# Eight of 16 shift tiles of the first norm by VectorE dots, in a hybrid attention layer on one Trainium2 core

## The chip, the cores and the metric

One core of a Trainium2 chip runs the whole layer in float32. The metric is device time in microseconds, the median of repeated runs. The engines named here are TensorE (PE in the profile; PEld is its weight load), VectorE (DVE), ScalarE (ACT), GpSimd (POOL) and SyncE (SP), whose queue issues nearly all DMAs.

## The reference

One layer over 256 latent tokens `x` and 256 context tokens `ctx`, width 2048. What matters here is the first norm and the projections that read it:

```python
mod = silu(c) @ w_mod + b_mod            # for x; 6 x 2048 columns
mod_c = silu(c_ctx) @ w_mod + b_mod      # for ctx
sh1, sc1, gt1, sh2, sc2, gt2 = split(mod, 6)
csh1, csc1, ... = split(mod_c, 6)
h  = rms_norm(x,   g_attn_pre) * (1 + sc1)  + sh1
hc = rms_norm(ctx, g_attn_pre) * (1 + csc1) + csh1
y  = mixer(h, hc)     # keys, values, queries, gates; window and neighbourhood attention; w_o
x  = x + gt1 * rms_norm(y, g_attn_post)
h  = rms_norm(x, g_ffn_pre) * (1 + sc2) + sh2
x  = x + gt2 * rms_norm(conv_ffn(h), g_ffn_post)
```

There are 10 key heads: 8 of the neighbourhood attention (B) and 2 of the window attention (A). In each, a query scores the latent keys and the context keys together in one softmax. A number added to all scores of a query does not change its softmax; so for a B head, whose keys are not rotated, a vector added to all latent and all context keys alike drops out.

## The kernel before

Features lie on partitions. `xn` holds x and ctx side by side, 16 feature tiles of 128 x 512 (256 latent tokens, 256 of the context). `hh` holds the normed tokens in two float32r parts, high and low (`h[:, 0]`, `h[:, 1]`). A weight block of 128 x 2048 goes from a `raw` buffer (four of them) into a high part `wh` (ScalarE) and a low part `wl` (VectorE), two buffers each; this is `split`, L141 and L145. A product is three matmuls: high by high, high by low, low by high.

**First key pass** (loop over the tiles k, pk of six heads). The scale of the norm is made as it goes: `narrow` multiplies silu(c) by scale tiles `rsc` (pm, L367), `scale_of` turns that into the gain columns `Gc` and the scaled `hh`. The keys are therefore of scaled tokens without shift and without the norm's own factor. `squares` adds up the squares; `pss` and `rstd_of` give the factor `rs`. `scaled_keys` (L306) multiplies the keys by it.

**Second key pass** (k = 0 to 15 again, pk of the last four heads). Weight units `ku` are loaded into `ru` and split, two tiles a unit. Beside it the shift is made, in two ways. `ND` = 4 feature tiles are dots on VectorE: `load_sd` loads a transposed 1 MB tile of `wm_sd` into the buffer `sd`, and `dot` (L481) multiplies it by a row of silu(c) or silu(c_ctx) and adds it up, two dots a tile; L485 adds the bias into `shc`. The first two dots stand in the first pass, at k = 12 and 14, six in the second. The other twelve tiles are a TensorE product `pmsh` (L597), at k = 1, 5, 9, 13, four tiles of `wm_sh` each, evacuated, transposed and added into `shc` at k = 14. At k = 15 TensorE turns `shc` (`ptsd`, L637), and it goes out to `shd`.

In the same pass `xn` is multiplied in place by Gc and rs (L610), and `whole` (L579, L580) then writes the final `hh`, with shift: tiles 0 to 2 inside the pass, the rest after it.

**Values** (L712). Ten weight blocks, four token tiles. Beside them VectorE has 29 dots (`beside`): 20 give the bias of the keys (two per head, L687: the shift of x and of ctx times the key weights `wkt`, a 1 MB block a head), and 9 are further columns of w_mod (`mods`, L244), whose rest follows in the attention, the gates and the output projection. `key_bias` (L673) adds the biases. The rows `shr` that these dots read are loaded from `shd` when the memory of the key passes is free, that is after the last `whole`.

**What sets the order.** The order of TensorE in both key passes is written by hand, and so is SyncE's until k = 12 of the first. All else is laid out by a planner before the run: each engine's queue is then fixed, and it takes the earliest piece of the code that is ready by the planner's own costs. A buffer is loaded again only when its last reader is done.

Of the kernel before, what the change touches and what calls it, by code (L numbers as in the profile page):

```python
# [10 lines left out]
F32 = mybir.dt.float32  # L11
F32R = mybir.dt.float32r
AF = mybir.ActivationFunctionType
ALU = mybir.AluOpType

P = 128
D = 2048
KT = D // P
S = 256
# [15 lines left out]
C_BMOD = 0  # L35
# [4 lines left out]
C_CW = 160  # L40
# [11 lines left out]
NBLK = B_DN + 44  # L52
NK1 = 6
NK2 = NKVA + NHB - NK1
ND = 4
SW = (KT - ND) * P // 4
KW = (NKVA + NHB) * P
J0, NS = 24, 8
# [13 lines left out]
def layer_kernel(ctx, tc, xc, xt, ccol, crow, wm_sc, wm_sd, wm_sh, wm_b, cols, wk, wkt, ws, rope, mask_a, bias_b, out):  # L72
# [46 lines left out]
    x1d = tc.dram_tile([S, D], F32, name="x1d")  # L119
    sild = tc.dram_tile([2 * KT, P], F32, name="sild")  # L120
    ggd = tc.dram_tile([2, KT, P], F32, name="ggd")
    shd = tc.dram_tile([2, D], F32, name="shd")

    nraw = [0]
    nmod = [0]
# [155 lines left out]
    with ExitStack() as mx:  # L281
# [10 lines left out]
        with ExitStack() as at:  # L292
# [30 lines left out]

            st = kv.enter_context(ExitStack())
            hcp = st.enter_context(tc.tile_pool(name="hcp", bufs=1))
            shc = hcp.tile([P, 2, KT], F32, name="shc")
            sp = st.enter_context(tc.tile_pool(name="sp", bufs=1, side="right"))
            xn = sp.tile([P, KT, T2], F32, name="xn")
            ssq = sp.tile([P, T2], F32, tag="ssq", bufs=1, name="ssq")
# [139 lines left out]

            def load_sd(t):  # L470
                if t < ND:
                    rsd[t] = sp.tile([P, D], F32, tag="sd", bufs=1, name=f"sd{t}")
                    sync.dma_start(out=rsd[t], in_=wm_sd[t])

            def dot(after=None):
                t, v = divmod(ndot[0], 2)
                ndot[0] += 1
                with ExitStack() as es:
                    if after:
                        es.enter_context(tc.issue_after(after))  # L480
                    d_ = nc.vector.scalar_tensor_tensor(  # L481
                        out=rsd[t][:] if v else junk, in0=rsd[t][:], scalar=1.0, in1=shrow[v], op0=ALU.mult, op1=ALU.mult,
                        accum_out=sh0[:, t, v : v + 1]).ins
                if v:
                    nc.vector.tensor_scalar(  # L485
                        out=shc[:, :, t], in0=sh0[:, t], scalar1=col[:, C_BMOD + t : C_BMOD + t + 1], scalar2=None, op0=ALU.add)
                    load_sd(t + 1)
                return d_

            def keys(pk, wh, wl, o, k, part=slice(0, 3)):  # L490
# [13 lines left out]
            for k in range(KT):  # L504
# [7 lines left out]
                        load_xn(3, 1)  # L512
                        load_sc(3)
                if k == 2:
                    cr = sp.tile([P, D], F32, tag="sd", bufs=1, name="cr")[: 2 * KT, :P]
                    sync.dma_start(out=cr, in_=crow)
                    nc.scalar.activation(cr, cr, AF.Silu)
                if k == 4:
                    sync.dma_start(out=sild, in_=cr)
                if k in (6, 8):  # L520
                    shrow.append(silu_row(wp, "wl", 2, (k - 6) // 2, F32R))
                if k == 10:
                    load_sd(0)
                if k >= KT - 2:
                    load_unit(k + 2)
                if k == 12:
                    sync.dma_start(out=col[:, C_CW:], in_=cols[:, C_CW:])
                    loads.close()
                if k > 3:
                    units[k + 1] = unit(k + 1)  # L530
                if k == 12:

                    d_ = dot(done_u[k + 1][1])
                    after = squares(14, done_u[k + 1][0], d_)
                    with tc.issue_after(sq_[0]):
                        warm_table(AF.Sqrt, "k", eps[:, 0:1])
                if k == 14:
# [45 lines left out]

            pm = bank("pmsh")
            pk = [acc(f"pk{NK1 + i}") for i in range(NK2)]
            rsh = {q: raw_block(wm_sh[q], (P, 4 * SW)) for q in range(4)}
            for k in range(KT):
                if k % 2 == 0:
                    load_unit(KT + k // 2 + 2)
                    if k + 2 < KT:  # L590
                        units[KT + k // 2 + 1] = unit(KT + k // 2 + 1)
                if k % 4 == 1:
                    keys(pk[0], *units[KT + k // 2], (k % 2) * NK2 * P, k)

                    for q in range(k - 1, k + 3):
                        for j in range(4):
                            nc.tensor.matmul(  # L597
                                pm[32 * j : 32 * j + 32, :SW], cc[:, q, :], rsh[q][:, SW * j : SW * j + SW],
                                start=q == 0, stop=q == KT - 1)
                    for q in range(k + 3, k + 7):  # L600
                        if q < KT:
                            rsh[q] = raw_block(wm_sh[q], (P, 4 * SW))
                if k == KT - 2:
                    split_to(b0)
                    load_to(b0 + 1)
                if k in (2, 3, 6, 7, 10, 11):
                    dot(e_.ins)
                for v in range(2):
                    x_ = xn[:, k, v * S : v * S + S]
                    nc.vector.scalar_tensor_tensor(  # L610
                        out=x_, in0=x_, scalar=Gc[:, k, v : v + 1], in1=rs[:, v * S : v * S + S],
                        op0=ALU.mult, op1=ALU.mult)
                if k > 12:
                    whole(k - 13)
                for i in range(k % 4 == 1, NK2):
                    keys(pk[i], *units[KT + k // 2], (k % 2) * NK2 * P + i * P, k)
                    if k == KT - 2 and i < 2:
                        if i == 0:
                            pt = bank("ptsh")
                        n_ = min(2 * P, SW - 2 * P * i)  # L620
                        ev = up.tile([P, 2 * P], F32, tag="half", bufs=2, name=f"evsh{i}")
                        nc.scalar.activation(ev[:, :n_], pm[:, 2 * P * i : 2 * P * i + n_], AF.Copy)
                        for b in range(0, n_, P):
                            o = 2 * P * i + b
                            nc.tensor.transpose(pt[:, o : o + P], ev[:, b : b + P], ident[:])
                        if i:

                            view = pt[:, :SW].rearrange("p (b j w) -> p j b w", j=4, w=32)
                            bm = col[:, C_BMOD + ND : C_BMOD + KT].rearrange("p (j b) -> p j b", j=4)
                            for v in range(2):  # L630
                                nc.vector.tensor_tensor(
                                    out=shc[:, v, ND:].rearrange("p (j b) -> p j b", j=4), in0=view[:, :, :, v], in1=bm,
                                    op=ALU.add)
                    if k == KT - 1 and i == 2:

                        pt = bank("ptsd")
                        nc.tensor.transpose(pt[: 2 * KT, :P], shc[:].rearrange("p a b -> p (a b)"), ident[:])  # L637
                        ev = up.tile([P, 2 * P], F32, tag="half", bufs=2, name="evsd")
                        nc.scalar.activation(ev[: 2 * KT, :P], pt[: 2 * KT, :P], AF.Copy)
                        sync.dma_start(out=shd.rearrange("v (k p) -> (v k) p", p=P), in_=ev[: 2 * KT, :P])  # L640
            order.close()
            for k in range(3, KT):
                if k in (3, 6):
                    for i in (0, 1) if k == 3 else (2, 3):
                        scaled_keys(NK1 + i, pk[i])
                whole(k)
            st.close()
            ccs.close()

# [10 lines left out]
            shr = []  # L660
            for v in range(2):
                shr.append((cbp, rowp)[v].tile([P, D], F32, tag="row", name=f"shr{v}"))
                sync.dma_start(out=shr[v], in_=shd[v].partition_broadcast(P))
            junk = cbp.tile([P, D], F32, name="junk")
            kb = cbp.tile([P, NKVA + NHB, 2], F32, name="kb")
            rkt = {}
            crb = [None]
            nbeside = [0]

            def key_bias(i):  # L670
                for v in range(2):
                    k_ = of(v, kT[:, i])
                    nc.scalar.activation(k_, k_, AF.Identity, bias=kb[:, i, v : v + 1])  # L673
                if i >= NHB:
                    rope_of(kT[:, i], 1, f"k{i}")

            def beside(n):
                for _ in range(n):
                    n_, v = divmod(nbeside[0], 2)
                    nbeside[0] += 1  # L680
                    if n_ < NKVA + NHB:
                        for q in range(n_, min(n_ + 2, NKVA + NHB)) if v == 0 else ():
                            if q not in rkt:
                                rkt[q] = raw_block(wkt[q])
                        i = n_
                        r = rkt[i]
                        nc.vector.scalar_tensor_tensor(  # L687
                            out=r if v else junk[:], in0=r, scalar=1.0, in1=shr[v][:], op0=ALU.mult, op1=ALU.mult,
                            accum_out=kb[:, i, v : v + 1])
                        if v and n_:  # L690
                            key_bias(n_ - 1)
                    else:
                        if crb[0] is None:
                            key_bias(NKVA + NHB - 1)
# [4 lines left out]
            for c, (n0, nw, per) in enumerate(((0, 512, 4), (512, 512, 4), (1024, 256, 8))):  # L699
                pv = [acc(f"pv{c}_{i}") for i in range(4)]  # L700
                for g in range(KT // per):
                    wh, wl = block(2)
                    for kk in range(per):

                        if nb and kk < (2 if nb == 8 else 3 if nb % 2 else 4):
                            beside(1)
                        k = g * per + kk
                        w = slice(kk * nw, kk * nw + nw)
# [849 lines left out]
```

## The time and the profile before

| | us |
|---|---|
| median of 3 runs (1499.41 to 1499.93) | 1499.61 |
| the profiled execution | 1500.27 |
| its span, first to last instruction | 1498.5 |
| TensorE busy | 1487.1 |
| VectorE busy | 1222.7 |
| ScalarE busy | 811.4 |
| shift product pmsh on TensorE (L597) | 11.1 |

Each row of the page gives an engine's busy time and its share of the span. The chain of waits goes back from the last instruction, at each step to what released it; an engine that owns the chain sets the time. The granted TensorE clock was 0.998. The longest stretches of the chain lie in the up projection (pu) and the down projection (c), which the change does not touch; it touches the first 270 us, and a little of the output projection (py_o, 677 to 765).

### The profile page before, as it was taken

What the parts mean: (1) busy time and instruction counts of PE and PEld (TensorE: products, weight loads), DVE (VectorE), ACT (ScalarE), POOL (GpSimd) and SP (SyncE); (2) the same over time, 40 slices, a digit from 0 to 9 for tenths busy, and PEclk for the clock granted to TensorE, in tenths of its full rate; (3) what the DMA queues carried; (4) which work ended last, traced back from release to release, by engine and by line L of the source; (5) the groups of instructions that cost most, each with busy time, mean ns of one, the idle gap of its engine ahead of it and who ended that gap; (6) DMA issues with size and microseconds to landing.
All of it is one profiled execution on the core that took longest, in us unless ns stands there. A gap on an engine that the chain in (4) does not pass through costs nothing.

```text
span 1498.5 us, 21727 instructions
## 1 busy us (share of the span) xinstructions
PE 1487.1 (99%) x8488; PEld 1279.0 (85%) x8488; DVE 1222.7 (82%) x1861; ACT 811.4 (54%) x1338; POOL 1.8 (0%) x11
## 2 busy tenths in 40 slices
PE   9999999999999999999999999999999999999997
PEld 7876889998888888888888888888888888888886
DVE  4496998989988888877778887887888878887887
ACT  4342542777765544555666555555555555445543
POOL 0000000000000000000000000000000000000000
PEclk9999999999999999999999999999999999999999
DMA  9988789754368888778856666666666654554652
GB/s 367 391 322 337 275 295 353 281 205 168 142 227 305 314 323 322 306 281 340 305 204 222 251 234 241 239 238 225 253 224 226 224 194 168 224 214 185 265 215 108
DMA packets 60551, 382.66 MB, mean 255 GB/s; under 512 B 6560, under 2 KB 8992, under 8 KB 18336
## 3 DMA queue, kind: packets, MB, share of 16 engines
q1 hardware_dynamic: 59728, 380.20, 67.5%
q8 instruction: 67, 1.10, 0.3%
q10 hardware_dynamic: 720, 1.07, 0.2%
q14 instruction: 36, 0.29, 0.1%
HBM read 377.00 MB, written 4.24 MB: 254 GB/s over the span
## 4 chain that ended last, share of the span: by engine, by line
PE 97%; DMA 1%; DVE 1%; ACT 1%; issue 0%; DVEq 0%
PE pu L214 21%; PE c L1318 12%; PE pu L215 11%; PE pk L493 7%; PE pv L712 7%; PE pg L214 7%; PE py_o L943 5%; PE pq L214 4%; PE pb L214 4%; PE pg L215 4%; PE x L1318 3%; PE pq L215 2%; PE pb L215 2%; PE po L853 1%; PE s L822 1%; PE pm L367 1%
## 5 line engine op out<-in xcount | busy, mean ns | idle before, releaser
L145 DVE TENSOR_TENSOR wl<-raw,wh 128x1024 fp32r<-128x1024 f32 (+1 forms) x444 | 520.6, 1201 | 114.3 <-ACT wh L141 113.7
L141 ACT ACTIVATE wh<-raw 128x1024 fp32r<-128x1024 f32 (+1 forms) x444 | 444.4, 1036 | 184.1 <-PE pg L214 54.5
L214 PE MATMUL pu<-h,wh 128*128 128x512 f32 x1404 | 487.6, 390 | 0.0
L215 PE MATMUL pu<-h,wl 128*128 128x256 f32 x1404 | 395.9, 282 | 0.0
L214 PEld LDWEIGHTS pu<-h,wh 128*128 128x128 f32 x1404 | 263.4, 188 | 55.0
L215 PEld LDWEIGHTS pu<-h,wl 128*128 128x128 f32 x1404 | 265.4, 189 | 0.0
L214 PE MATMUL pg<-h,wh 128*128 128x512 f32 x464 | 161.5, 390 | 0.0
L1318 PE MATMUL c<-wh,ff 128*128 128x512 f32 x448 | 138.0, 389 | 0.0
L215 PE MATMUL pg<-h,wl 128*128 128x256 f32 x464 | 130.8, 282 | 0.0
L493 PE MATMUL pk<-h,ku 128*128 128x512 f32 x480 | 118.0, 398 | 0.6 <-DVE ku L145 0.4
L244 DVE SCALAR_TENSOR_TENSOR raw<-raw,crb 128x2048 f32<-128x2048 f32 x48 | 109.6, 2285 | 9.8 <-DMA raw<-in_wm_b_dram 9.3
L219 ACT ACTIVATE half_u<-pu 128x256 f32<-128x256 f32 x88 | 33.6, 384 | 147.8 <-PE pu L215 147.8
L493 PEld LDWEIGHTS pk<-h,ku 128*128 128x128 f32 x480 | 87.4, 188 | 25.3 <-issue 4.8
L214 PE MATMUL pq<-h,wh 128*128 128x512 f32 x304 | 108.7, 396 | 0.0
L214 PEld LDWEIGHTS pg<-h,wh 128*128 128x128 f32 x464 | 87.1, 188 | 18.2
L712 PE MATMUL pv<-wh,h 128*128 128x512 f32 (+1 forms) x384 | 101.6, 354 | 0.0
L1318 PEld LDWEIGHTS c<-wh,ff 128*128 128x128 f32 x448 | 84.1, 188 | 17.4
L214 PE MATMUL pb<-h,wh 128*128 128x512 f32 x256 | 89.4, 390 | 0.0
L215 PEld LDWEIGHTS pg<-h,wl 128*128 128x128 f32 x464 | 87.7, 189 | 0.0
L1318 PE MATMUL c<-wl,ff 128*128 128x512 f32 x224 | 87.3, 390 | 0.0
L215 PE MATMUL pq<-h,wl 128*128 128x256 f32 x304 | 85.5, 281 | 0.0
L943 PE MATMUL py_o<-wh,zz 128*128 128x512 f32 x256 | 78.4, 390 | 0.0
(241 smaller groups left out, 2085.8 us busy)
## 6 DMA issues: line engine op xcount, KB each, us to landing
raw<-in_ws_dram SPq DMA_DIRECT2D x222, 1024.0 KB, 4.8
raw<-in_wm_b_dram SPq DMA_DIRECT2D x64, 1024.0 KB, 4.8
raw<-in_wm_sc_dram SPq DMA_DIRECT2D x15, 1024.0 KB, 7.8
raw<-in_wm_sh_dram SPq DMA_DIRECT2D x16, 768.0 KB, 7.1
raw<-in_wkt_dram SPq DMA_DIRECT2D x10, 1024.0 KB, 6.9
raw<-in_wk_dram SPq DMA_DIRECT2D x7, 768.0 KB, 8.3
crb<-sild SPq DMA_DIRECT2D x4, 1024.0 KB, 7.7
sd<-in_wm_sd_dram SPq DMA_DIRECT2D x4, 1024.0 KB, 8.4
```

Source lines behind the costliest of these rows:

```text
L141: a_ = nc.scalar.activation(hi, src, AF.Copy)
L145: v_ = nc.vector.tensor_tensor(out=lo, in0=src, in1=hi, op=ALU.subtract)
L214: nc.tensor.matmul(pt[:, :], wh[:, w], a, start=first and i == 0, stop=False, skip_group_check=True)
L215: nc.tensor.matmul(pt[:, :S], wl[:, w], a[:, 0], start=False, stop=last and i == n - 1, skip_group_check=True)
L219: a_ = nc.scalar.activation(t[:], pt[:, S:], AF.Copy)
L244: nc.vector.scalar_tensor_tensor(out=r, in0=r, scalar=1.0, in1=row, op0=ALU.mult, op1=ALU.mult, accum_out=modx[:, j : j + 1])
L367: nc.tensor.matmul(pm[32 * j : 32 * j + 32, t * P : t * P + P], cc[:, q, :], rsc[k + t][:, q * P : q * P + P], start=q < 4, stop=q >= KT - ...
L493: nc.tensor.matmul(pk[:], wt[:, w], hh[:, :, k, a], start=k == 0 and a == 0 and wt is wh, stop=k == KT - 1 and a == 1)
L712: nc.tensor.matmul(pv[i][:, :nw], src[:, k, a, t0 : t0 + P], wt[:, w], start=k == 0 and q == 0, stop=k == KT - 1 and q == 2)
L822: nc.tensor.matmul(s_ps, qs[hd][:, a, qt * P : qt * P + P], k_[:, w], start=q == 0, stop=q == 2)
L943: p_ = nc.tensor.matmul(py[t][:], act[:, k, a, t * P : t * P + P], wt[:, w], start=k == 0 and q == 0, stop=k == nk - 1 and q == 2)
L1318: nc.tensor.matmul(pt[:], a(i), wt[:, w], start=k not in begun, stop=stop and q == 2, skip_group_check=True)
```

## The change

- `ND` = 8: eight tiles of the shift are dots, and `pmsh` has 256 columns in place of 384. `sd` has two buffers. Tile 0 is loaded at k = 9 of the first pass, tile 1 at 13, tile 2 before the second pass, and each further tile when the second dot of the tile two before is done. The dots stand at k = 10 (two) and k = 14 of the first pass, and one at each k from 0 to 12 of the second.
- Shift tiles of `wm_sh` are loaded two at a time, 1 MB a load. The load of `cols` moves from k = 12 of the first pass to k = 8 of the second.
- `xn` is multiplied by Gc on ScalarE (two instructions of 256) and by rs on VectorE (one of 512).
- Block 1 of the values is split after whole(9), and not after the last `whole`.
- `shc` and `shd` get a third row: the context's shift less the latent one. B heads get one dot, with this row, and one bias, on the context's keys; A heads keep two dots, the second now with the difference, and the first result is added to it.
- Beside the values are 25 dots: 12 for the keys and 13 of `mods`.

```diff
-ND = 4
+ND = 8
...
-            shc = hcp.tile([P, 2, KT], F32, name="shc")
+            shc = hcp.tile([P, 3, KT], F32, name="shc")
...
-                    rsd[t] = sp.tile([P, D], F32, tag="sd", bufs=1, name=f"sd{t}")
+                    rsd[t] = sp.tile([P, D], F32, tag="sd", bufs=2, name=f"sd{t}")
...
-                    load_sd(t + 1)
+                    if t:
+                        load_sd(t + 2)
...
-                if k == 10:
-                    load_sd(0)
+                if k in (9, 13):
+                    load_sd(k // 13)
...
                 if k == 12:
-                    sync.dma_start(out=col[:, C_CW:], in_=cols[:, C_CW:])
                     loads.close()
...
+                if k == 10:
+                    dot(dot(done_u[k + 1][1]))
                 if k == 12:
-                    d_ = dot(done_u[k + 1][1])
-                    after = squares(14, done_u[k + 1][0], d_)
+                    after = squares(14, *done_u[k + 1])
...
-            rsh = {q: raw_block(wm_sh[q], (P, 4 * SW)) for q in range(4)}
+            rsh = {}
+            def load_sh(k):
+                for q in range(k, min(k + 4, KT), 2):
+                    r = raw_block(wm_sh[q : q + 2].rearrange("k p n -> p k n"), (P, 2, 4 * SW))
+                    rsh[q], rsh[q + 1] = r[:, : 4 * SW], r[:, 4 * SW :]
+            load_sh(0)
+            load_sd(2)
             for k in range(KT):
+                if k == 8:
+                    sync.dma_start(out=col[:, C_CW:], in_=cols[:, C_CW:])
...
-                    for q in range(k + 3, k + 7):
-                        if q < KT:
-                            rsh[q] = raw_block(wm_sh[q], (P, 4 * SW))
+                    load_sh(k + 3)
...
-                if k in (2, 3, 6, 7, 10, 11):
+                if k < 13:
                     dot(e_.ins)
                 for v in range(2):
                     x_ = xn[:, k, v * S : v * S + S]
-                    nc.vector.scalar_tensor_tensor(
-                        out=x_, in0=x_, scalar=Gc[:, k, v : v + 1], in1=rs[:, v * S : v * S + S],
-                        op0=ALU.mult, op1=ALU.mult)
+                    nc.scalar.activation(x_, x_, AF.Copy, scale=Gc[:, k, v : v + 1])
+                nc.vector.tensor_tensor(out=xn[:, k], in0=xn[:, k], in1=rs[:], op=ALU.mult)
...
-                        nc.tensor.transpose(pt[: 2 * KT, :P], shc[:].rearrange("p a b -> p (a b)"), ident[:])
+                        nc.vector.tensor_tensor(out=shc[:, 2], in0=shc[:, 1], in1=shc[:, 0], op=ALU.subtract)
+                        nc.tensor.transpose(pt[: 3 * KT, :P], shc[:].rearrange("p a b -> p (a b)"), ident[:])
...
                 whole(k)
+                if k == 9:
+                    split_to(b0 + 1)
...
-                sync.dma_start(out=shr[v], in_=shd[v].partition_broadcast(P))
+                sync.dma_start(out=shr[v], in_=shd[2 * v].partition_broadcast(P))
...
-                for v in range(2):
+                for v in range(2) if i >= NHB else (1,):
                     k_ = of(v, kT[:, i])
                     nc.scalar.activation(k_, k_, AF.Identity, bias=kb[:, i, v : v + 1])
...
+            jobs = [(i, v) for i in range(NKVA + NHB) for v in ((1,) if i < NHB else (0, 1))]
...
+                        if v and i >= NHB:
+                            nc.vector.tensor_tensor(out=kb[:, i, 1:], in0=kb[:, i, 1:], in1=kb[:, i, :1], op=ALU.add)
...
-                        if nb and kk < (2 if nb == 8 else 3 if nb % 2 else 4):
+                        if nb and kk < (2 if nb > 7 else 3):
                             beside(1)
```

More of the change, by code (lines that the diff above doesn't have):

```diff
@@ L121, in layer_kernel @@
     ggd = tc.dram_tile([2, KT, P], F32, name="ggd")
-    shd = tc.dram_tile([2, D], F32, name="shd")
+    shd = tc.dram_tile([3, D], F32, name="shd")
     nraw = [0]
@@ L485, in dot @@
                     nc.vector.tensor_scalar(
-                        out=shc[:, :, t], in0=sh0[:, t], scalar1=col[:, C_BMOD + t : C_BMOD + t + 1], scalar2=None, op0=ALU.add)
-                    load_sd(t + 1)
+                        out=shc[:, :2, t], in0=sh0[:, t], scalar1=col[:, C_BMOD + t : C_BMOD + t + 1], scalar2=None, op0=ALU.add)
+                    if t:
+                        load_sd(t + 2)
                 return d_
@@ L514, in layer_kernel @@
                 if k == 2:
-                    cr = sp.tile([P, D], F32, tag="sd", bufs=1, name="cr")[: 2 * KT, :P]
+                    cr = sp.tile([P, D], F32, tag="sd", bufs=2, name="cr")[: 2 * KT, :P]
                     sync.dma_start(out=cr, in_=crow)
@@ L616, in layer_kernel @@
                     keys(pk[i], *units[KT + k // 2], (k % 2) * NK2 * P + i * P, k)
-                    if k == KT - 2 and i < 2:
+                    if k == KT - 2 and i < -(-SW // (2 * P)):
                         if i == 0:
@@ L625, in layer_kernel @@
                             nc.tensor.transpose(pt[:, o : o + P], ev[:, b : b + P], ident[:])
-                        if i:
+                        if i == -(-SW // (2 * P)) - 1:
                             view = pt[:, :SW].rearrange("p (b j w) -> p j b w", j=4, w=32)
@@ L636, in layer_kernel @@
                         pt = bank("ptsd")
-                        nc.tensor.transpose(pt[: 2 * KT, :P], shc[:].rearrange("p a b -> p (a b)"), ident[:])
+                        nc.vector.tensor_tensor(out=shc[:, 2], in0=shc[:, 1], in1=shc[:, 0], op=ALU.subtract)
+                        nc.tensor.transpose(pt[: 3 * KT, :P], shc[:].rearrange("p a b -> p (a b)"), ident[:])
                         ev = up.tile([P, 2 * P], F32, tag="half", bufs=2, name="evsd")
-                        nc.scalar.activation(ev[: 2 * KT, :P], pt[: 2 * KT, :P], AF.Copy)
-                        sync.dma_start(out=shd.rearrange("v (k p) -> (v k) p", p=P), in_=ev[: 2 * KT, :P])
+                        nc.scalar.activation(ev[: 3 * KT, :P], pt[: 3 * KT, :P], AF.Copy)
+                        sync.dma_start(out=shd.rearrange("v (k p) -> (v k) p", p=P), in_=ev[: 3 * KT, :P])
             order.close()
@@ L667, in layer_kernel @@
             crb = [None]
-            nbeside = [0]
             def key_bias(i):
-                for v in range(2):
+                for v in range(2) if i >= NHB else (1,):
                     k_ = of(v, kT[:, i])
@@ L675, in key_bias @@
                     rope_of(kT[:, i], 1, f"k{i}")
+            jobs = [(i, v) for i in range(NKVA + NHB) for v in ((1,) if i < NHB else (0, 1))]
             def beside(n):
                 for _ in range(n):
[L679 to L682, printed above, removed]
+                    if jobs:
+                        i, v = jobs.pop(0)
+                        for q in range(i, min(i + 2, NKVA + NHB)):
                             if q not in rkt:
                                 rkt[q] = raw_block(wkt[q])
-                        i = n_
                         r = rkt[i]
@@ L689, in beside @@
                             accum_out=kb[:, i, v : v + 1])
-                        if v and n_:
-                            key_bias(n_ - 1)
+                        if v and i >= NHB:
+                            nc.vector.tensor_tensor(out=kb[:, i, 1:], in0=kb[:, i, 1:], in1=kb[:, i, :1], op=ALU.add)
+                        if v and i:
+                            key_bias(i - 1)
                     else:
```

## The prediction

> **What bounds the kernel now.** I read the page first (engine totals, chain), then the chain piece by piece around the first norm, then busy time by stretch, then VectorE's own timeline, then the loads.
>
> ```profile
> span 1498.5 us, 21727 instructions
> PE 1487.1 (99%) x8488; PEld 1279.0 (85%) x8488; DVE 1222.7 (82%) x1861; ACT 811.4 (54%) x1338; POOL 1.8 (0%) x11
> PE 97%; DMA 1%; DVE 1%; ACT 1%; issue 0%; DVEq 0%
> ```
>
> TensorE is busy for 99% of the span and owns 97% of the chain. So a gain must be TensorE work removed, and a loss must be a new TensorE wait. The sum is against this profiled execution: span 1498.5, 1500.27 us with what lies around it; the median of the three runs is 1499.61, so I add my change to the median.
>
> The chain, in order of time (start, us, what):
>
> ```profile
> 100.79 2.72 PE pmsh L597 x32
> ...
> 153.05 0.11 PE ptsd L637
> 153.16 0.70 PE pk L493 x3
> 153.87 110.09 PE pv L712 x576
> ```
>
> The shift product (pmsh) is four groups of 32 records, 2.72 us each; the first is shown. The second key pass ends and the values begin at 153.87.
>
> Busy time by stretch (TensorE, weight load, VectorE, ScalarE, GpSimd, clock, DMA share, GB/s):
>
> ```profile
> 60.00:80.00 20.00, 20.00 (x203) 16.25 (x202) 9.92 (x20) 9.83 (x17) 0.00 (x0) 1.00 1.01 413
> 88.60:101.25 12.65, 12.65 (x62) 10.05 (x64) 12.65 (x19) 2.98 (x3) 0.00 (x0) 1.00 0.87 328
> 101.25:149.81 48.56, 48.16 (x289) 33.66 (x281) 37.06 (x64) 12.35 (x18) 0.00 (x0) 1.00 0.87 338
> 153.90:263.90 110.00, 110.00 (x577) 95.04 (x576) 97.87 (x108) 42.99 (x73) 0.46 (x2) 1.00 0.83 311
> ```
>
> Four things are to be seen: TensorE waits 0.4 us in the second key pass (48.16 of 48.56); in 60 to 80 the DMA engines are full; VectorE has no gap from 88.6 to 101.25; from there to 149.81 it has 48.56 - 37.06 = 11.5 us to spare. That is what the change spends.
>
> **What it removes from TensorE.** The nearest group of narrower records, in the chain:
>
> ```profile
> 71.60 1.89 PE pm L367 x64
> ```
>
> A group of 32 records takes 2.72 us at 384 columns, and half of a 64-record group takes 0.94 at 128; straight between them, 256 columns take 1.83, so 0.89 a group, 3.6 us for four. One transpose goes (0.11, as ptsd's). The 0.4 us wait may go. Bound: -4.1 us, if nothing new waits.
>
> **What it adds to VectorE in the second key pass.** Durations from start to start in its timeline:
>
> ```profile
> 68.48 0.69 DVE L433 TENSOR_TENSOR ssq<-ssq,sq 128x512 f32<-128x512 f32 x1
> 69.09 0.95 DVE L145 TENSOR_TENSOR ku<-raw,ku 128x768 fp32r<-128x768 f32 x1
> 74.76 0.47 DVE L388 TENSOR_SCALAR Gc<-ptm,col,bgc 128x2 f32<-128x2 f32 x2 [4.72 <-PE ptm L386]
> ...
> 101.25 1.67 DVE L610 SCALAR_TENSOR_TENSOR xn<-xn,Gc,rs 128x256 f32<-128x256 f32 x4
> 102.84 2.29 DVE L481 SCALAR_TENSOR_TENSOR kT<-sd,crb 128x2048 f32<-128x2048 f32 x1
> 105.05 0.08 DVE L481 DVE_READ_ACCUMULATOR kT<-sd,crb 128x1 f32 x1
> ...
> 108.05 1.22 DVE L145 TENSOR_TENSOR ku<-ru,ku 128x1024 fp32r<-128x1024 f32 x1
> 109.19 0.23 DVE L485 TENSOR_SCALAR shc<-sh,col 128x2 f32<-128x2 f32 x1
> 109.32 0.48 DVE L610 SCALAR_TENSOR_TENSOR xn<-xn,Gc,rs 128x256 f32<-128x256 f32 x1
> ```
>
> A dot is 2.21, its column add 0.13, an xn product of 256 is 0.40, a sum of two 512-wide tiles 0.61 (68.48 to 69.09; the nearest row for the new xn product), a 1024-wide split 1.14 (108.05 to 109.19), which is also a wl half. In the second pass there are 13 dots instead of 6: 7 x 2.21 = 15.5; four more column adds: 0.5; 32 products of 0.40 become 16 of 0.61: -3.0; the subtraction for the third row, 0.13, priced as a column add. whole(3), two products of the xn kind and size, ran ahead into this stretch and now falls behind it, as its place in the code says: -0.8. Together +12.3, against 11.5 spare. The stretch ends with the last adds into shc:
>
> ```profile
> 149.65 0.24 DVE L631 TENSOR_TENSOR shc<-ptsh,col 128x12 f32<-128x12 f32 x2 [1.85 <-PE ptsh L625]
> ```
>
> Without one idle moment its work now ends at 101.25 + 37.06 + 12.3 = 150.6.
>
> Who waits for its end: TensorE's order is written by hand, and the ptsd transpose (last unit but one of the pass) reads shc, which needs the last dot and the subtraction. Without a wait TensorE would be there at 153.05 - 4.1 = 148.9. Two more splits can stand ahead of the subtraction: block 0's wl halves, at k = 14 in the code, the subtraction at k = 15. Before, their weights had to wait until the last shift loads freed a buffer; now two 1 MB loads hold what four buffers held, so the weights can come earlier. With both halves ahead the subtraction ends at 152.9, with none at 150.6. I take one, 151.7, for the order is not to be seen before it is laid out. From ptsd to the first value product is 153.87 - 153.05 = 0.82.
>
> **What it does to TensorE in the first key pass.** Tile 0 of wm_sd moves from k = 10 to k = 9, ahead of the xn loads and of scale tiles 12 and 13, in a queue order written by hand:
>
> ```profile
> 52.48 0.52 SPq L250 DMA_DIRECT2D crb<-sild  x1
> 53.05 0.97 SPq L340 DMA_DIRECT2D xn<-in_xc_dram  x2
> ```
>
> Scale tiles 12 and 13 by issue and landing:
>
> ```profile
> L134 SPq DMA_DIRECT2D raw<-in_wm_sc_dram x1: 327/327/327, 59.3 to 59.3; - x1
> ...
> DMA to landing us min/median/max: 9.2/9.2/9.2
> ...
> L134 SPq DMA_DIRECT2D raw<-in_wm_sc_dram x1: 328/328/328, 61.9 to 61.9; - x1
> ...
> DMA to landing us min/median/max: 9.1/9.1/9.1
> ```
>
> They land at 68.5 and 71.0, over 9 us after issue and 2.5 us apart for 1 MB: with the engines full, this queue is bound by bytes, and comes out in order of issue. With 1 MB more ahead, tile 12 lands at 71.0 and tile 13 at 73.5. TensorE needs them at 71.60 and 72.54 (half of the 1.89). So a new wait of about 1.0 us at 72.5, which moves all behind it, pss and VectorE's chain from 88.6 too. Its bounds: 0, if the engines take the loads otherwise, and 2.5, if tile 13 had no slack. [...]
>
> The two dots that now stand at k = 10 cost 4.55 in VectorE's 4.72 us gap before 74.76: hidden, and the wait just named widens the gap; without that cover they would push Gc by 4.55.
>
> **The sum.** Values begin at 151.7 + 1.0 + 0.8 = 153.5, against 153.87: -0.4. Of the 4.1 us saved, 1.0 goes to the load and some 2.7 to ptsd's wait on VectorE.
>
> **Edits at nothing.** ScalarE's 32 extra scalings at 0.40 (VectorE's own xn price) make 12.8 us beside 12.35 busy in 48.56. The cols load moves to k = 8; its first reader there is far behind. Splitting block 1 after whole(9) puts two wl halves 2.3 us earlier among 13 x 0.8 us of whole; TensorE takes 11 us a block (110.09 for ten). Four dots fewer beside the values remove 4 x 2.2 from a VectorE that had 12 us spare and made TensorE wait for nothing in 153.9 to 263.9. But shr's second row now gates the first dot, and its load waits for the last whole, on the VectorE that is now behind; before, in the first of these rows, VectorE idled 3.5 us there for the first row:
>
> ```profile
> 172.39 2.29 DVE L687 SCALAR_TENSOR_TENSOR junk<-raw,shr 128x2048 f32<-128x2048 f32 x1 [3.52 <-DMA shr<-shd]
> 223.40:264.40 41.00, 41.00 (x274) 37.91 (x273) 33.59 (x34) 11.90 (x19) 0.00 (x0) 1.00 0.90 342
> ```
>
> Eight dots now take a fresh 1 MB block each, so a group of values loads four blocks: 4 x 2.5 = 10 us of 11. The stretch from 223.4 in the second row, where each wm_b dot reads a fresh block, is already such a one, and TensorE is busy for all of its 41 us. Four wm_b dots and loads leave the output projection, whose products are in the 99%; nothing is booked. So 1499.61 - 0.4 = 1499.2.
>
> **Rivals.** *VectorE keeps up.* Its order lets the subtraction through in time, because my 0.61 is too dear or work I put ahead of it falls behind. Then only the load's wait stands against the saving: -4.1 + 1.0 = -3.1, 1496.5; without that wait 1495.5. For it: ScalarE idles, and VectorE's order is free to change. Against: 12.3 us in 11.5. Chance 0.25.
>
> *wm_sd comes too late.* With two buffers, a slot is refilled while the other tile's two dots run: 2 x (2.21 + 0.61) + 1.14 + 2 x 0.13 + 0.61 = 7.65 us. The two loads of before in that stretch:
>
> ```profile
> L473 SPq DMA_DIRECT2D sd<-in_wm_sd_dram x2: 328/328/328, 108.2 to 122.1; - x2
> ...
> DMA to landing us min/median/max: 7.4/8.4/9.5
> ```
>
> Five tiles (3 to 7) come so. At 8.4 each waits 0.75, 3.7 in all: 1499.2 + 3.7 = 1502.9, slower; at 9.5 it would be 9. It decides above 8.3 us a load. For it: two of the three loads of a group are still queued behind shift loads. Against: those are 2 MB a group instead of 3, and xn products can fill the gap. Chance 0.15.
>
> *The values become load-bound.* At the 311 GB/s of the values before 4.19 MB take 13.5 us, 2.5 over a block; for three groups +7.5, 1506.7. Against: 413 GB/s were moved from 60 to 80. Chance 0.05. [...]
>
> **How the numbers follow.** Forecast 0.55: VectorE's chain takes back most of the saving; its own range is -2.9 to +2.9 (no half to both halves ahead, the load's wait 0 to 2.5, up to 1 us of idle in the chain). 0.2% is 3.0 us, about what a measurement of this kernel can tell from no change. Faster 0.25, same 0.55, slower 0.20. The range reaches to the first rival's 1495.5 and the second's 1502.9.
>
> **What would show it.** After: a pmsh group of 1.8 us; a TensorE gap near 72.5 ended by a raw load; VectorE without idle time from 88.6 to the subtraction; ptsd waiting 2 to 4 us for it; the first value product near 153.5. I am wrong if ptsd waits under 1 us, if VectorE idles on sd, or if TensorE waits for a wl in the values.

## The result, and the profile after

The changed kernel takes 1509.84 us (median of 4 runs, 1508.79 to 1510.29), the kernel before 1499.51 beside it: a ratio of 1.0068, 95% interval 1.0051 to 1.0085. It is slower by 10.3 us, where I had forecast 1499.2. The profiled execution took 1510.29, with a span of 1508.5.

First the page of the changed kernel, as at the head of the prediction (engine totals, granted TensorE clock in 40 slices, chain):

```profile
span 1508.5 us, 21740 instructions
PE 1488.5 (99%) x8487; PEld 1281.9 (85%) x8487; DVE 1220.8 (81%) x1852; ACT 821.4 (54%) x1361; POOL 1.8 (0%) x11
PEclk9999999899999999999999999999999999999999
PE 92%; DVE 4%; DMA 2%; ACT 1%; issue 1%; DVEq 0%
```

TensorE has less work, and yet it is busy 1.4 us longer: in slice 8 of 40 its clock is not whole. And 8% of the chain are not its own, where it was 3%. The same stretches as before the change:

```profile
60.00:80.00 20.00, 19.17 (x198) 15.31 (x197) 13.60 (x23) 10.35 (x20) 0.00 (x0) 1.00 1.02 414
101.25:149.81 48.56, 46.17 (x294) 33.95 (x293) 48.44 (x61) 15.71 (x26) 0.00 (x0) 1.00 0.91 354
153.90:263.90 110.00, 110.00 (x577) 95.05 (x576) 91.81 (x109) 36.22 (x56) 0.46 (x2) 1.00 0.88 338
223.40:264.40 41.00, 41.00 (x274) 37.93 (x273) 33.14 (x30) 9.90 (x14) 0.00 (x0) 1.00 1.00 402
```

TensorE has the wait in 60 to 80, and one of 2.4 us in the second key pass, where VectorE is now full (48.44 of 48.56). In the values it waits for nothing (110.00 of 110.00), but the DMA engines are full from 223.4 on: 402 GB/s, share 1.00, where it was 342 and 0.90. TensorE's rows at these places:

```profile
73.48 1.08 PE L367 MATMUL pm<-raw,cc 128*32 128x128 f32 x32 [0.83 <-DMA raw<-in_wm_sc_dram]
...
140.98 2.00 PE L608 MATMUL pmsh<-raw,cc 128*32 128x256 f32 x32
142.91 2.56 PE L494 MATMUL pk<-h,ku 128*128 128x512 f32 x10
147.87 0.73 PE L494 MATMUL pk<-h,ku 128*128 128x512 f32 x2 [2.39 <-DVE ku L145]
...
152.77 0.62 PE L724 MATMUL pv<-wh,h 128*128 128x512 f32 x2
...
153.90 0.27 PE L646 MATMUL ptsd<-ident,shc 128*48 128x128 f32 x1
...
263.68 0.39 PE L214 MATMUL pq<-h,wh 128*128 128x512 f32 x1
...
271.73 0.50 PE L214 MATMUL pq<-h,wh 128*128 128x512 f32 x1 [2.33 <-ACT wh L141]
272.99 0.53 PE L215 MATMUL pq<-h,wl 128*128 128x256 f32 x1 [0.76 <-DVE wl L145]
...
284.25 0.48 PE L856 MATMUL pt<-ident,sma 128*128 128x128 f32 x1 [2.96 <-DVE sma L849]
```

Up to the end of the values little is lost: the first query product starts at 263.68, and before the change at 263.80:

```profile
263.80 0.39 PE L214 MATMUL pq<-h,wh 128*128 128x512 f32 x1
```

The whole loss arises in the next 27 us, where the queries take over from the values: 2.33 + 0.76 us of waiting for block 11, 2.96 for the first head's softmax, and behind each gap a stretch at half clock:

```profile
147.80:151.00 3.20, 3.13 (x15) 2.58 (x16) 3.20 (x8) 2.02 (x5) 0.00 (x0) 1.00 1.00 415
272.90:276.50 3.60, 3.52 (x11) 3.03 (x12) 3.60 (x5) 0.24 (x1) 0.00 (x0) 0.53 0.29 89
284.30:290.00 5.70, 5.70 (x18) 4.62 (x19) 5.46 (x7) 5.25 (x10) 0.00 (x0) 0.50 0.48 168
```

3.6 us at 0.53 lose 1.7, 5.7 us at 0.50 lose 2.85 (a 512-column product takes 0.43 us there and 0.23 ahead of the gap): with the 6.05 of gaps 10.6, which is the whole loss and a little more. (Behind the 2.39 us wait at 147.87 the clock stayed at 1.00.)

Why the first gap? ScalarE's timeline, the kernel before and then the changed one:

```profile
263.28 0.74 ACT L717 ACTIVATE vv<-pv 128x256 f32<-128x256 f32 x2
263.92 1.05 ACT L141 ACTIVATE wh<-raw 128x1024 fp32r<-128x1024 f32 x1
264.87 0.38 ACT L717 ACTIVATE vv<-pv 128x256 f32<-128x256 f32 x1
265.13 1.06 ACT L141 ACTIVATE wh<-raw 128x1024 fp32r<-128x1024 f32 x1
...
269.56 0.39 ACT L764 ACTIVATE qb<-pq 128x256 f32<-128x256 f32 x1 [2.85 <-PE pq L215]
...
272.88 1.28 ACT L109 ACT_TABLE_LOAD   x1
```

```profile
262.80 1.46 ACT L729 ACTIVATE vv<-pv 128x256 f32<-128x256 f32 x4 [7.71 <-PE pv L724]
269.44 0.38 ACT L776 ACTIVATE qb<-pq 128x256 f32<-128x256 f32 x1 [5.17 <-PE pq L215]
270.31 0.42 ACT L141 ACTIVATE h<-rq 128x256 fp32r<-128x256 f32 x1 [0.49 <-DVE rq L777]
270.63 1.99 ACT L141 ACTIVATE wh<-raw 128x1024 fp32r<-128x1024 f32 x2
...
281.49 1.28 ACT L844 ACT_TABLE_LOAD   x1
282.79 0.64 ACT L844 ACTIVATE sma<-sma,st 128x416 f32<-128x416 f32 x1
...
283.43 1.99 ACT L141 ACTIVATE wh<-raw 128x1024 fp32r<-128x1024 f32 x2
```

(Blocks are numbered from 0; 0 to 9 are the values', 10, 11 and 12 those of the first three queries.) Before, block 11's split (`wh`, 263.92) stands among the copies of the last values. Now it stands behind `qb`, the copy of the first query, which must wait for TensorE until 269.44; ScalarE idles 5.17 us. Block 12's split (283.43) stands behind the first head's exponential, ahead of which ScalarE loads the table (1.28 us at 281.49, on the path; before, 1.28 at 272.88, in idle time). Yet the two blocks had long landed. Their loads in the trace, before and then after:

```profile
L134 SPq DMA_DIRECT2D raw<-in_ws_dram x1: 327/327/327, 250.7 to 250.7; - x1
...
DMA to landing us min/median/max: 8.8/8.8/8.8
```

```profile
L134 SPq DMA_DIRECT2D raw<-in_ws_dram x1: 328/328/328, 252.9 to 252.9; - x1
...
DMA to landing us min/median/max: 7.6/7.6/7.6
```

Block 11 landed at 259.5 before the change and at 260.5 after. Block 12 was issued at 264.4 before and at 261.0 after; it landed at 270.3 and at 270.5:

```profile
L134 SPq DMA_DIRECT2D raw<-in_ws_dram x1: 328/328/328, 264.4 to 264.4; - x1
...
DMA to landing us min/median/max: 5.9/5.9/5.9
```

```profile
L134 SPq DMA_DIRECT2D raw<-in_ws_dram x1: 350/350/350, 261.0 to 261.0; - x1
...
DMA to landing us min/median/max: 9.5/9.5/9.5
```

So what changed is the order that the planner wrote for ScalarE. Why it wrote this one is not shown; it goes by its own costs, not by the landings above.

### The profile page after: what moved, and what is told of

Same layout as the page of the kernel before. It is cut to its first block, busy times and chain, and to the rows that moved or that the text cites. A ratio compares the mean times of both kernels' runs of the same rounds, so it can differ in the third digit from the quotient of the medians.

```text
span 1508.5 us, 21740 instructions
## 1 busy us (share of the span) xinstructions
PE 1488.5 (99%) x8487; PEld 1281.9 (85%) x8487; DVE 1220.8 (81%) x1852; ACT 821.4 (54%) x1361; POOL 1.8 (0%) x11
## 4 chain that ended last, share of the span: by engine, by line
PE 92%; DVE 4%; DMA 2%; ACT 1%; issue 1%; DVEq 0%
PE pu L214 21%; PE c L1330 12%; PE pu L215 11%; PE pv L724 7%; PE pg L214 7%; PE py_o L955 6%; PE pq L214 5%; PE pb L214 4%; PE pg L215 4%; PE pk L494 3%; PE x L1330 3%; PE pq L215 2%; PE pb L215 2%; PE po L865 1%; PE s L834 1%; PE pt L856 1%
## 5 line engine op out<-in xcount | busy, mean ns | idle before, releaser
L214 PE MATMUL pq<-h,wh 128*128 128x512 f32 x304 | 112.5, 406 | 2.3 <-ACT wh L141 2.3
```

What stands on the lines that cost most here:

```text
L214: nc.tensor.matmul(pt[:, :], wh[:, w], a, start=first and i == 0, stop=False, skip_group_check=True)
```

## The experiments

Theory 1: the 25 dots beside the values read 23 fresh 1 MB blocks (10 of keys, 13 of mods), where the 29 read 19, and this makes the hand-over late. Rival 2: the key passes do it. Rival 3: ScalarE's fixed order is the price, not the loads. Rival 4: it is VectorE's work. (The expectation of e9 calls rival 3 theory 3. Theory 5 and rival 6 are about the clock, rival 7 about the loads of the second key pass.) Each ratio is against runs of the kernel before taken beside it, with medians of 1499.2 to 1499.7.

**Which half of the change.** Passes alone (e1: the changed kernel with the old `key_bias`, job list and counts), values alone (e2: the old kernel with a third row in `shc` and `shd`, and the new dots).

> Both key passes as in the changed kernel (ND = 8, sd0 at k = 9, narrower pmsh), but beside the values the 29 dots of before, two for every B head. Theory 1 (the 25 dots of the values, with three fresh 1 MB blocks a group, make the value and query weights late; the passes are worth -0.3): 1499.2, within 1 us of before, and no TensorE gap over 1 us between 263 and 290. Rival 2 (the passes, or the shift of times that they bring, make the hand-over late): about 1509, with the gaps near 270 and 281 still there.

> The passes of before (ND = 4, pmsh of 384 columns) with the third shift row, and the changed kernel's 25 dots beside the values. Theory 1: the whole loss without the passes, about 1510 (1508 to 1512), gaps near 270 and 281. Rival 2: about 1499.6, no such gaps. If both halves are needed at once, both this and the passes alone stay near 1499.5.

Passes alone: 1501.02, ratio 1.0012 (1.0003 to 1.0020). Values alone: 1507.84, ratio 1.0055 (1.0043 to 1.0068), with waits of 1.42, 0.76 and 2.97 us at the hand-over. So theory 1 holds against rival 2 for some 8 of the 10 us. The passes alone miss their 1499.2 by 1.8 us, but in the profiled execution (1500.42) the passes are not what is late: the first query product starts at 263.06, 0.7 us earlier than before. What they gain goes at the hand-over again, in waits of 0.29 and 1.17 us for block 12, where no gap over 1 us was expected:

```profile
277.42 0.38 PE L215 MATMUL pq<-h,wl 128*128 128x256 f32 x1 [1.17 <-DVE wl L145]
```

There too the block had landed (at 272.5), and its split came at 274.65, behind the second query's copy at 274.37.

**Bytes or dots.** e3 leaves four mods to later, e5 keeps 25 dots but loads fewer blocks, e11 keeps the loads without the dots:

```diff
# e3
-                        if nb and kk < (2 if nb > 7 else 3):
+                        if nb and kk < (1 if nb == 9 else 2 if nb > 4 else 3):
...
# e5; the first of two heads that share a block leaves it unchanged
-                                rkt[q] = raw_block(wkt[q])
+                                rkt[q] = rkt[q - 1] if q % 2 and q < NHB else raw_block(wkt[q])
...
# e11, on top of e3
+                        elif nb and kk < (2 if nb > 7 else 3):
+                            spare.append(raw_block(wkt[0]))
+                            if len(spare) > 1:
+                                nc.vector.tensor_copy(junk[:, :1], spare.pop(0)[:, :1])
...
```

> The changed kernel with 21 dots beside the values instead of 25: two a block from block 5 on and one beside block 9, so four fresh 1 MB blocks fewer in the second half of the values. Theory 1 (bytes make weight blocks 11 and 12 late): 4 MB fewer, some 10 us of loads, so blocks 11 and 12 land in time, both gaps go, 1499 to 1501. Rival 3 (ScalarE's fixed order at the hand-over and not the loads): the order stays, the first gap stays, 1505 to 1510.

> The changed kernel with all its 25 dots, but two neighbourhood heads share one 1 MB key block, so that 19 fresh blocks are loaded beside the values as before, not 23 (left out: half of the heads get the wrong block's bias). Theory 1 (bytes make weight blocks 11 and 12 late): 1499 to 1501, as with 21 dots, though VectorE does as much as in the changed kernel. Rival 4 (VectorE's dots in the values, not the loads, are what got dearer, and 21 dots helped by being fewer): about 1509.

> The kernel with 21 dots beside the values, and in the place of the four dots that it leaves out only their four 1 MB loads, read by copies of one column (VectorE has no more to do than with 21 dots). Theory 1 (fresh blocks that pass through the raw buffers make the hand-over late): the whole loss comes back, 1507 to 1510, with the gaps near 270 and 281. Rival 4 (VectorE's dots): 1499.

21 dots: 1499.05, ratio 0.9998 (0.9989 to 1.0007). 25 dots on 19 blocks: 1499.29, ratio 0.9999 (0.9990 to 1.0008). 21 dots and 4 spare loads: 1511.48, ratio 1.0076 (1.0064 to 1.0089), the whole loss. The spare loads' stretch of values:

```profile
223.40:263.90 40.50, 40.50 (x272) 37.57 (x271) 26.03 (x27) 9.90 (x14) 0.00 (x0) 1.00 1.00 398
```

VectorE has 7 us less to do there than in the changed kernel, TensorE waits for nothing, and the DMA engines are full: rival 4 falls. So does rival 3 as e3 had it, an order that stays whatever is loaded. But look at what 25 dots on 19 blocks change, in its ScalarE timeline:

```profile
264.65 1.10 ACT L729 ACTIVATE vv<-pv 128x256 f32<-128x256 f32 x3 [7.95 <-PE pv L724]
265.65 1.05 ACT L141 ACTIVATE wh<-raw 128x1024 fp32r<-128x1024 f32 x1
```

Its load, and the time that the loads of that stretch took:

```profile
L134 SPq DMA_DIRECT2D raw<-in_ws_dram x1: 327/327/327, 253.3 to 253.3; - x1
...
DMA to landing us min/median/max: 8.2/8.5/8.8
```

Block 11 landed no sooner than 261.5, later than in the changed kernel, and its split still runs in time, since it stands at its old place. So it isn't the landing. The loads act through the order: that joins theory 1 and rival 3.

**The order alone.** e4 puts only the first query's `qb` behind block 11's split, e9 also the second `qb` and the first head's exponentials behind block 12's:

```diff
# e4; e9 likewise with ahead[1], taken behind the second fill(0)
+                        with ExitStack() as es:
+                            if hd == order[0]:
+                                es.enter_context(tc.issue_after(ahead[0]))
+                            nc.scalar.activation(t[:], pq[:, S:], AF.Copy, scale=SCALE)
...
             fill(0)
+            ahead = last[:]
...
```

> The changed kernel, same loads; only the first query's copy qb on ScalarE is put behind block 11's split (wh11), so that the split may run as soon as its block has landed (260.5 in the changed kernel). Rival 3 (ScalarE's order): the first gap (2.3 + 0.8 us near 270) and the half clock behind it (1.7) go, 1505; the second gap (3.0 near 281 and 2.6 of half clock), which hangs on block 12's landing at 270.5, stays. Theory 1 in its strict form (bytes alone): block 11 has landed long before, so also a gain here, but block 12 decides: 1505 to 1510.

> The changed kernel with its 25 dots and 23 fresh blocks. On ScalarE, block 11's split is ahead of the first query's copy, and block 12's split ahead of the second query's copy and the first head's exponentials; the warming of the exponential table is then ahead of them too. Theory 3 (the fixed order at the hand-over is the whole price, late blocks only bring it about): block 11 landed at 260.5 and block 12 at 270.5 in the changed kernel, both before they are needed (269.4 and 281.3), so both gaps and both stretches of half clock go: 1499.2, 10 us better than the changed kernel. Theory 1 in its strict form (the blocks themselves are too late for TensorE): some 2 to 5 us stay, 1502 to 1504.

e4: 1504.40, ratio 1.0031 (1.0020 to 1.0041), the first gap is gone, as rival 3 said (1505). e9: 1502.02, ratio 1.0016 (1.0007 to 1.0025). With all 23 blocks loaded, the order gives back 7.8 of the 10.3. What is left shows in e9's TensorE timeline and windows:

```profile
279.95 0.39 PE L215 MATMUL pq<-h,wl 128*128 128x256 f32 x1 [1.79 <-DVE wl L145]
```

```profile
149.00:152.40 3.40, 3.40 (x10) 2.68 (x9) 3.40 (x8) 2.23 (x6) 0.00 (x0) 0.52 0.90 373
```

A wait for block 12's low half, which I had not moved on VectorE, and, in this execution, a half clock behind the 2.11 us wait of the second key pass: its values end 1.8 us later than the changed kernel's, which is no part of the hand-over. The 1502 is also what theory 1 in its strict form forecast, but not by late blocks: block 12's high half was done by 274.5 and VectorE stood idle for 4.15 us until 277.39, with the softmax ahead of the low half in its order. So rival 3 is right in what it names and forecast 3 us too little.

**The half clock.** e6 fills the first gap with small products, in the order of the changed kernel:

```diff
...
+                    if half == 0 and len(todo) == NH + 1:
+                        keep_busy(18, "h", pq)
...
```

> The changed kernel, same order on all engines, with 18 small products of the identity on TensorE between the first and the second query block, where it stands idle 2.3 us; they take about 2.0 us at 0.11 each. Theory 5 (the idle time brings the granted clock down to half, which costs 1.6 us behind this gap on top of it): the 512-column products behind it take 0.23 and not 0.43, time 1508.2. Rival 6 (the half clock has another cause, or comes from the second piece of the gap, 0.76): 1509.8 or more. The gap near 281 and its half clock stay in both.

1507.83, ratio 1.0053 (1.0041 to 1.0066): 2.0 us less than the changed kernel. Behind the filled gap the clock is whole:

```profile
272.40:276.00 3.60, 3.60 (x24) 3.20 (x23) 3.60 (x5) 0.22 (x1) 0.00 (x0) 1.00 0.35 96
```

So here it was the idle time that brought the half clock: 0.53 with the gap, 1.00 with it filled. The 2.0 us are not its price: the filling took 3.96 us (2.0 expected), more than the gap, and in this execution the second gap's half clock lasted only half as long as the 6.8 us of the changed kernel. The price of the first is the 1.7 us read above.

**The second key pass.** The prediction had TensorE wait there for VectorE. In the changed kernel VectorE does hold up the last key unit: ScalarE's part of it is done by 144.8, and VectorE, which has no idle moment there, comes to it at 146.60.

```profile
143.78 1.06 ACT L141 ACTIVATE ku<-ru 128x1024 fp32r<-128x1024 f32 x1 [0.35 <-DMA ru<-in_wk_dram]
```

```profile
146.60 1.22 DVE L145 TENSOR_TENSOR ku<-ru,ku 128x1024 fp32r<-128x1024 f32 x1
```

Whether that makes the time was tried on the kernel with 21 dots: half the xn product (e7), a quarter of the xn products on GpSimd (e8), VectorE's order (e10), wm_sd on GpSimd's queue (e12).

```diff
# e7
-  nc.vector.tensor_tensor(out=xn[:, k], in0=xn[:, k], in1=rs[:], op=ALU.mult)
+  nc.vector.tensor_tensor(out=xn[:, k, :S], in0=xn[:, k, :S], in1=rs[:, :S], op=ALU.mult)
...
# e8
+  eng = nc.gpsimd if k % 4 == 2 else nc.vector
...
# e10, round the last xn products and whole's low parts
+  with tc.issue_after(done_u[KT + 7][1]):
...
# e12
-  sync.dma_start(out=rsd[t], in_=wm_sd[t])
+  (sync if t < 2 else nc.gpsimd).dma_start(out=rsd[t], in_=wm_sd[t])
```

> The kernel with 21 dots, in which VectorE multiplies by rs only the latent half of xn (256 columns instead of 512, 16 times; left out: the context's factor). VectorE's chain in the second key pass gets about 16 x 0.25 = 4 us shorter. The prediction's step (VectorE is late in the second key pass and TensorE waits for it, 2.5 us here): those waits near 141 to 147 go, 1496.5. Rival (the wait hangs on the shift loads or the TensorE order, VectorE only happens to be last): 1498.5 to 1499.

> The kernel with 21 dots, full computation, four of the 16 products of xn with rs (k = 2, 6, 10, 14) on GpSimd, which is idle there. VectorE's chain gets 4 x 0.61 = 2.4 us shorter. If GpSimd works beside VectorE without slowing it: the waits near 141 to 147 go down to under 0.7, 1497. If the two engines disturb each other, or GpSimd takes several us for one product, which no run shows so far: 1499 or above.

> The kernel with 21 dots, full computation; in VectorE's order the last xn products and all low parts of the final h stand behind the split of the last key unit. In the kernel with 21 dots ScalarE's part of that split ended near 144.3, VectorE's began only at 146.04 and TensorE waited 1.5 us for it. If VectorE's order makes that wait: it falls to 0.5 as before the change, 1498. If it hangs on the unit's load or on ScalarE: 1499, no change.

> The kernel with 21 dots, full computation; wm_sd tiles 2 to 7 are issued by GpSimd and no longer by SyncE, whose in-order queue stood still for them until a dot had set a buffer free (the last one was issued at 130.98 in the changed kernel, with the last shift loads at 131.4 and 131.9 and the last key unit at 132.4 right behind it). In every kernel with ND = 8 so far TensorE's waits for the last shift load and the last key unit add up to 2.1 to 2.6 us (without GpSimd's products), whatever VectorE had to do. If the queue's order makes these two loads late: they land some 1.5 to 2 us sooner, the waits go down to about 0.7, and the gap can no longer halve the clock: 1497. If bytes or VectorE's own chain bind: 1499, as with 21 dots; if the two queues share the engines badly: over 1500.

1499.26, 1502.65, 1499.23 and 1500.21 (ratios 0.9997, 1.0020, 1.0000 and 1.0000, each +-0.0009). Only e8 moves, upwards. The wait moves too: in e7 and e10 the planner or I put other work elsewhere, and TensorE waits 0.87 + 1.18 for key units, or 1.35 for a shift load and 0.76 for a unit. With the unit put ahead on VectorE (e10) the two waits add up to 2.1 us, with 21 dots alone to 2.0 (0.52 + 1.51): VectorE's order says which wait it is, not how long both are. In e12 wm_sd takes longer (8.6 us in the median, 5.6 in the changed kernel), VectorE idles 4.1 us from 95 to 150 (1.27 and 0.46 of it listed as waits for wm_sd), and three units come late (waits of 0.89, 0.49 and 1.16). So I took the two suspects, VectorE's dots and the loads, apart, on e10: half the dots with all the loads (e13), full dots with four wm_sd loads fewer (e14). Neither computes the layer any more; they show only what the waits hang on.

```diff
# e13, with the output cut alike
-  in0=rsd[t][:], scalar=1.0, in1=shrow[v],
+  in0=rsd[t][:, : D // 2 if t > 1 else D], scalar=1.0, in1=shrow[v][:, : D // 2 if t > 1 else D],
...
# e14
+  if 3 < t < ND:
+      rsd[t] = rsd[t - 2]
```

> The kernel with 21 dots and the last key unit's split ahead on VectorE; the dots of tiles 2 to 7 take only 1024 of 2048 columns (left out: half of each sum), all loads as they are. VectorE's work in the second key pass falls by 12 x 1.1 = 13 us, far below what the pass has. The prediction's step (VectorE is the bound there): TensorE's waits between 95 and 150 fall from 2.1 to 2.6 us to under 0.7, 1497. Rival 7 (the loads are the bound: the last shift load and the last key unit land at 142 to 144 whatever VectorE does): the waits stay over 1.5 us, 1499.

> The same kernel with full dots, but tiles 4 to 7 of wm_sd are not loaded (left out: their dots read what the two buffers hold), 4 MB fewer in the second key pass; VectorE does all it did. Rival 7 (loads): the last loads land some 8 us sooner, the waits fall under 0.7, 1497. The prediction's step (VectorE): the waits stay at 2 us or more, 1499.

1497.10, ratio 0.9981 (0.9972 to 0.9990), and 1495.90, ratio 0.9975 (0.9965 to 0.9984). Both take the wait away. The stretch from 95 to 150, of e13 and then of e14:

```profile
95.00:150.00 55.00, 54.77 (x334) 41.52 (x334) 43.81 (x74) 17.54 (x27) 0.00 (x0) 1.00 0.89 345
```

```profile
95.00:150.00 55.00, 55.00 (x337) 42.04 (x336) 55.00 (x74) 16.62 (x27) 0.00 (x0) 1.00 0.73 269
```

e14 is the telling one: VectorE has not one idle moment (55.00 of 55.00), and TensorE has none either. A full VectorE, as I had predicted it, does not by itself hold TensorE up here. And e13 loads the same bytes, at 345 GB/s, so lack of bandwidth alone doesn't either. What both shorten is the loop between them: a wm_sd buffer comes free by a dot, SyncE's queue stands still until then, and the shift load and the key unit behind it land late. In the changed kernel the dot that ends at 130.9 lets the last wm_sd tile go at 130.98, and the last key unit goes at 132.41; in e13 these are 125.38 and 129.53, and in e14 the unit goes at 129.43 and lands in 5.8 us instead of 11.3. That the loop is the cause is the reading that fits both; no edit with the whole computation has shown it. The last try keeps the whole computation and issues the key units one earlier:

```diff
-  tag="sq", bufs=2
+  tag="sq", bufs=3
...
+  load_unit(KT + 2)
...
-  load_unit(KT + k // 2 + 2)
+  load_unit(KT + k // 2 + 3)
```

> The kernel with 21 dots, full computation; the key units of the second key pass have three buffers instead of two and are loaded one unit earlier, so that the last unit's 1 MB (0.5 MB a tile) is issued ahead of the last wm_sd tile and of the last two shift loads. If the waits of the second key pass come from loads that are issued late, behind dots that must first set a buffer free (as half the dots and fewer loads both took them away): the last unit's wait goes, the last shift load's stays at 0.5 to 1, sum under 1.0 instead of 2.1 to 2.6, the gap no longer halves the clock, 1497.5. If VectorE's order still puts the unit's split late, or the engines are full anyway: 1499, as with 21 dots.

1499.26, ratio 0.9998 (0.9989 to 1.0007): no change. The unit's wait went, and the last shift load's grew:

```profile
143.69 1.07 PE L609 MATMUL pmsh<-raw,cc 128*32 128x256 f32 x16 [1.76 <-DMA raw<-in_wm_sh_dram]
```

```profile
145.40:148.40 3.00, 3.00 (x9) 2.32 (x8) 3.00 (x8) 0.91 (x2) 0.00 (x0) 0.50 0.96 399
```

Another order of the loads moves the wait; only less work in the loop removed it. No version with the whole computation came out faster than the kernel before by more than can be measured; the nearest are the change with 21 dots (e3) and this last one, both at a ratio of 0.9998.

## Why the prediction was wrong, point by point

- **TensorE's saving** was nearly right: a pmsh group takes 1.93 us (140.98 to 142.91; forecast 1.83), so 3.2 us for four instead of 3.6.
- **The load's wait in the first key pass** was right in place, cause and size: 1.1 us at 72.4 between the products of scale tiles 12 and 13 (0.83 of it listed as idle; forecast 1.0). The DMA engines moved 414 GB/s from 60 to 80, by which 1 MB takes 2.5 us (an estimate), the step between two landings that the forecast took; the 402 GB/s over the 41 us at the end of the values are near it.
- **VectorE in the second key pass** was nearly right in its arithmetic: it has 48.44 of 48.56, and the subtraction stands behind both wl halves, at 153.33 (152.9 + 1.0 by the upper bound; I took 152.7):

```profile
153.33 0.17 DVE L645 TENSOR_TENSOR shc<-shc 128x16 f32<-128x16 f32 x1
```

  Its consequence was wrong: ptsd does not wait at all, since the planner put five value products ahead of it and of the last three key products (152.77 to 153.90), so the hand-written order does not hold to the end of the pass. TensorE's 2.39 us wait is for the last key unit instead. VectorE has a part in it, but e10, e13 and e14 speak for the loop of dots, buffers and loads behind it and against a full VectorE as such. That the size is near the forecast 2.7 is luck.
- **The sum up to the values** held at their end, -0.1 against -0.4, by those errors and by luck. The range of -2.9 to +2.9 counts the -0.4 twice: the terms named for it give -2.5 to +3.3. The measured +10.3 lies outside of both.
- **"Edits at nothing" is the step that failed.** There I checked the four loads a group against TensorE within the values, found 10 of 11 us covered, and booked nothing. That check holds: no wait in 110 us. But it looked only at the stretch itself. The four loads more changed the planner's order on ScalarE for the 27 us behind it, and there 6.05 us of gaps and 4.6 of half clock arose. With four loads fewer (e3) both were gone; with the loads and another order on ScalarE (e9) most of it was. Whoever stands behind the covered stretch, and in which order, was not asked; nor had I any price for a TensorE gap but its own length.
- **Rivals.** "The values become load-bound" (0.05) had the right resource (the DMA engines, at a share of 1.00 from 223.4 on), with the wrong mechanism (a wait in the values) and the wrong price (+7.5). "VectorE keeps up" and "wm_sd comes too late" did not happen: VectorE was full, and the wm_sd loads of the second pass took 5.6 us in the median and 7.7 at most, where the rival needed over 8.3. Of my three signs of being wrong, the first came true (ptsd waits under 1 us), and a wait for a wl came too, only 9 us behind the values and not in them.

## What to carry to other kernels

Loads that fit under a stretch are not free for that (here 110 us of values without a wait, and 10.3 us lost behind them): look at what the next stretch needs first, and at which instruction the engine that takes it will stand when it arrives (here ScalarE idled 5.17 us at a copy, with block 11 landed). Where a planner fixes the order, compare the order of the engines before and after at every hand-over; here ScalarE's order alone held 7.8 of the 10.3 us, though one block had landed 1.0 us later than before and the next 0.2. And price a TensorE gap of two to three us not at its length alone: a stretch at half clock can come with it, here some 1.7 us a stretch and once 2.85.

## What was not expected of the hardware

A TensorE gap can bring a stretch of half clock that is longer than the gap. The windows above show the stretches only roughly; worked out from the granted clock of half-microsecond windows, they last 3.4 us behind 2.33 + 0.76 (273.1 to 276.5), behind 2.11 in e9 (149.1 to 152.5) and behind 1.76 in e15 (145.1 to 148.6), and twice that, 6.8, round the 2.96 (283.3 to 290.1). A stretch is not sure to come, and the gap's length does not decide it: the clock fell behind 1.76 (e15) and 2.11 us (e9), and stayed at 1.00 behind 1.51 (e3) and 2.39 (the changed kernel). With such a wait near 146, one execution of e3 differs from the next by 2 us (1498.4 to 1500.6); that the clock makes this difference is not shown. A stretch of 3.4 us takes about 0.001 off the mean clock of an execution (an estimate: half of 3.4 in 1500), and the mean clock is known in thousandths: in e9 the four shortest executions (1500.2 to 1501.1) have 0.999 and the other seven 0.997 or 0.998, but in e3 0.998 and 0.999 stand among the shorter and the longer times alike. What sets a stretch's length, and which gap brings one, these runs do not show.
